# One post-norm transformer-like layer on one core: parameter load, table transposes, buffer slots, step order and last tile rearranged

## The chip, the cores and the metric

The kernel runs on one NeuronCore of one Trainium2 chip. The metric is the device time of one execution in microseconds; the time before is 1027.43 us, the median of three runs (1026.75 to 1028.75). Lower is better. All arithmetic is float32; large products are made from float32r parts (a value split in a high part and a residual, three matmuls for one product).

## The reference, cut to what matters

```python
h = x @ w_in                                  # 1024 x 1024 times 1024 x 2048, split in u, q, k, v, gate
bu = einsum(u, b_bar); states = associative_scan(lam_bar, bu)      # S5: 32 groups, 64 complex states
y  = gelu(Re(C . states) + d * u); y_s5 = rms_norm(y * sigmoid(y @ glu_w + glu_b))
y_ret = group_norm(retention(rotary(q), rotary(k), v)) * silu(gate)  # 4 heads, chunks of 64
x1 = layer_norm(alpha * x + concat(y_s5, y_ret) @ w_out)
a, g = split(x1 @ w_up); a = causal_conv3(a) + conv_b
out = layer_norm(alpha * x1 + (silu(a) * g) @ w_down)              # 1024 x 2816 times 2816 x 1024
```

The sequence has 1024 positions, the width is 1024, the channel mixer's inner width 2816.

## The kernel before, in words

The whole layer is one Python function that issues instructions to five engines: T (TensorE, "PE" in the profile), V (VectorE, DVE), S (ScalarE, ACT), G (GpSimd, POOL) and SP (the queue that issues nearly all DMAs). A planner orders each engine's instructions ahead of time: at each point of its own modelled run it takes the earliest instruction in program order whose inputs are ready, so an instruction can stand ahead of one that is earlier in the code. On the chip each engine then works through its list strictly in that order, with semaphores for the dependencies.

**Buffers.** Most SBUF tiles come from an arena of 20 narrow slots (2048 words per partition) and 2 wide ones. `A.get` takes the slot that was freed longest ago, `A.free` puts one at the end of the list. A tile in a used slot can be written only when every access to the tile that had the slot before is over. PSUM has eight banks, given out in turn by `bank`; `small` gives the same bank again as long as nothing else took one.

**First projection and S5 tables.** `project(blk, ...)` multiplies x by one quarter of w_in: four pairs `kp`, each loaded and split by `load_w` (lines 181 to 189: ACT makes the high part, DVE the residual), 24 matmuls per k-block. Block 0 gives u in eight banks; lines 286 to 295 copy u to U0 and U1 on ACT and store them to DRAM (`uscr`, line 294) in four DMAs; `load_UT` (line 299) reads them back transposed. Beside this DVE works out the S5 tables from the parameters: par3 (steps and eigenvalues, line 277) is loaded by `load_constants`, which `project(0)` calls after its second pair. Lines 326 to 407 are a long chain of small DVE operations on 32 to 256 columns; lines 421 to 423 make W0 and W1 from two products and a sum each, 2048 columns wide. Line 491 loads d over a part of `par` that line 422 reads.

**The second projection (v).** `project(2, ...)` multiplies by the block of v with seven banks, and between its matmuls it takes steps from a list, one per matmul: in the first two k-blocks (42 matmuls) eight `make_BT` steps, one every five matmuls, each with four transposes of W (line 451) into the one bank of `small` and a copy on ACT into BT0 or BT1 (line 452); in the next two eight `make_V` steps (line 465) with BT and UT. wsp2_0 and wsp2_1, the weights of the first two pairs, get their slots ahead of time; wsp2_2 takes whatever slot is next.

**Retention, gated unit, output product.** Lines 945 to 983 write the order of the steps by hand as strings: letter and block number. y is the S5 output, s, o, n and t the retention's scores, output, norm and transpose, a, m and b the gated unit's transposes in, product and transposes out, w the output product's retention part, F and f the two parts of the output product for blocks 4 to 7, p its second part for blocks 0 to 3. s, o, m, b, a, t, w, F take one to three banks each, in that order.

**Last product.** Line 1314 on: the second half of the output (zw[1], four tiles) is normalized by `layer_norm_far` on DVE while PE multiplies the last quarter for the four tiles of zw[0]: 33 matmuls of 512 columns for each tile, then line 1322 adds, and the tile is normalized. Tiles 0 and 1 use `layer_norm` (DVE, then ACT for the scale and GpSimd for adding the bias, line 867), tiles 2 and 3 `layer_norm_last` (two DVE operations of 512 columns, line 891, each with its own DMA). Each norm takes the power of the variance on GpSimd (line 860).

Of the kernel before, what the change touches and what calls it, by code (L numbers as in the profile page):

```python
# [12 lines left out]
F32 = mybir.dt.float32  # L13
F32R = mybir.dt.float32r
I32 = mybir.dt.int32
AF = mybir.ActivationFunctionType
ALU = mybir.AluOpType
# [3 lines left out]
P = 128  # L21
# [7 lines left out]
EPS = 1e-5  # L29
# [6 lines left out]
S_B1, S_B2, S_C1, S_C2, S_LRE, S_LIM, S_LS, S_END = 0, 512, 1024, 1536, 2048, 2080, 2112, 2144  # L36
# [70 lines left out]
def layer_kernel(ctx, tc, a, out):  # L107
    nc = tc.nc
    V, S, G, T, SP = nc.vector, nc.scalar, nc.gpsimd, nc.tensor, nc.sync

    cp = ctx.enter_context(tc.tile_pool(name="cp", bufs=1))
# [3 lines left out]
    A = Arena(ap_, 20, 2)  # L115
# [5 lines left out]
    def bank(name, keep=None):  # L121
        bank_n[0] += 1
        while bank_n[0] % 8 in kept.values():
            bank_n[0] += 1
        if keep is not None:
            kept[keep] = bank_n[0] % 8
        return ps.tile([P, 512], F32, tag=f"ps{bank_n[0] % 8}", name=name)
# [4 lines left out]
    def mm3(o, lh, ll, rh, rl, first, last):  # L132
        T.matmul(o, lhsT=lh, rhs=rh, start=first, stop=False)  # L133
        T.matmul(o, lhsT=lh, rhs=rl, start=False, stop=False)  # L134
        T.matmul(o, lhsT=ll, rhs=rh, start=False, stop=last)  # L135
# [31 lines left out]
    ahead_w = {}  # L167
# [27 lines left out]
    def project(blk, ops, banks, between=(), after=None, mid=None):  # L195


        ws = []
        late = len(between) > 0
        for kp in range(4):  # L200
            with tc.high_priority(0 if blk == 0 else HP):
                w, n = load_w(blk, kp)
            todo = deque(between[kp]) if late and kp < 2 else deque()
            ws.append(w)
            for q in range(2):
                k = 2 * kp + q
                if k < 7:
                    for (xi_, wi_) in ((0, 0), (0, 1), (1, 0)):
                        for j in range(7 if late and kp < 2 else 8):
                            l, r = ops(w[:, q], k, j, xi_, wi_)  # L210
                            T.matmul(banks[j], lhsT=l, rhs=r, start=(k == 0 and xi_ == 0 and wi_ == 0), stop=False)  # L211
                            if todo:
                                todo.popleft()()
                else:
                    for j in range(8):
                        proj3(banks[j], ops, w[:, q], k, j, False, True)
            assert not todo
            if mid is not None and kp == 1:
                mid()
            if late and kp < 2:  # L220
                if kp == 0:
                    continue
                if after is not None:
                    after()
                banks[7] = small("late")
                for k in range(4):
                    wk = ws[k // 2][:, k % 2]
                    proj3(banks[7], ops, wk, k, 7, k == 0, False)
                A.free(f"wsp{blk}_0")
            A.free(n)  # L230
            if blk == 3:
                A.free(f"x{2 * kp}", f"x{2 * kp + 1}")
# [11 lines left out]
    def spread_out(groups, n):  # L244

        return [g for gr in groups for g in [gr] + [lambda: None] * (n - 1)]
# [24 lines left out]
    banks = [bank(f"u{j}") for j in range(8)]  # L271
    par = A.get([P, 2048], F32, "par")
    pw = A.get([P, 2048], F32, "pw")
    par3 = pw[:, 1600:1696]

    def load_constants():
        SP.dma_start(par3, a["s5p"][:, 2048:S_END])
        SP.dma_start(con, a["con"])
        SP.dma_start(ident, a["ident"])
        SP.dma_start(par, a["s5p"][:, 0:2048])  # L280
        SP.dma_start(gains, a["gains"])
# [90 lines left out]
    l2, t5, kr, ki = tmp32(), tmp32(), tmp32(), tmp32()  # L372
# [40 lines left out]
    def vec_b(t, lo):  # L413
        return cust(t, lo * 16, [[16, 16], [0, 8], [1, 16]])

    A.free("scr")
    W = []
    for h in range(2):
        w_ = A.get([P, 16, 8, 16], F32, f"W{h}")
        t_ = A.get([P, 16, 8, 16], F32, f"Wt{h}")  # L420
        V.tensor_mul(w_, rev_pow(KR, 16 * h), vec_b(par[:, S_B1:S_B1 + 512], 16 * h))
        V.tensor_mul(t_, rev_pow(KIs, 16 * h), vec_b(par[:, S_B2:S_B2 + 512], 16 * h))
        V.tensor_add(w_, w_, t_)
        A.free(f"Wt{h}")
        W.append(w_)

    UT = []
    for h in range(2):
        UT.append(load_UT(h, f"UT{h}"))
        A.free(f"U{h}")  # L430

    scan = A.get([P, 4, 2, 256], F32, "scan")
    t1s = [scan[:, h] for h in range(2)]
# [13 lines left out]
    def make_BT(q):  # L447
        b_ = small(f"bt{q}")
        for e in range(4):
            g = 4 * q + e  # L450
            T.transpose(b_[:, e * P:(e + 1) * P], W[g // 16][:, g % 16].rearrange("p j c -> p (j c)"), ident)
        S.copy(BT[q // 4][:, 4 * (q % 4):4 * (q % 4) + 4], b_.rearrange("p (g k) -> p g k", g=4))
# [8 lines left out]
    def make_V(i):  # L461
        h, q = i // 4, i % 4
        b_ = small(f"v{h}{q}")
        for e in range(4):
# [4 lines left out]


    banks = [bank(f"v_{b}") for b in range(7)] + [None]
    project(2, ops_b, banks, [spread_out([partial(make_BT, q) for q in range(8)], 5),
                              spread_out([partial(make_V, i) for i in range(8)], 5)])
    A.free("BT0", "BT1", "UT0", "UT1")
    vt = [A.get([P, 4, 512], F32, f"vt{h}") for h in range(2)]
# [10 lines left out]
    def short_kernel(g):  # L486
        T.matmul(kb[:, 16 * g:16 * g + 16], lhsT=W[g // 16][:, g % 16].rearrange("p j c -> p (j c)"),
                 rhs=c1s[:, 16 * g:16 * g + 16], start=True, stop=True)
# [78 lines left out]
    banks = [bank(f"qk{b}") for b in range(7)] + [None]  # L567
# [28 lines left out]
    def glu_weights():  # L596
        r = A.get([P, 4, 512], F32, "glr")
        SP.dma_start(r, a["glu_w"])
        glh = A.get([P, 4, 512], F32R, "glh")
        gll = A.get([P, 4, 512], F32R, "gll")  # L600
        for k in range(4):
            S.copy(glh[:, k], r[:, k])
            V.tensor_sub(gll[:, k], r[:, k], f32(glh[:, k]))
        A.free("glr")
        return glh, gll

    glw = []
    banks = [bank(f"g_{b}") for b in range(8)]
    project(3, ops_b, banks, mid=lambda: glw.extend(glu_weights()))
    glh, gll = glw  # L610


# [124 lines left out]
    mh = cp.tile([P, 1], F32, name="mh")  # L737
# [125 lines left out]
    def layer_norm(z, lnv, pool, i):  # L863
        mv, rs = norm_stats(z, pool, i)
        V.scalar_tensor_tensor(z, z, mv[:, 0:1], lnv[:, 0], ALU.subtract, ALU.mult)
        S.activation(z, z, AF.Copy, scale=rs)  # L866
        G.tensor_add(z, z, lnv[:, 1])  # L867
# [18 lines left out]
    def layer_norm_last(z, lnv, pool, i, after):  # L886
        mv, rs = norm_stats(z, pool, i)
        V.scalar_tensor_tensor(z, z, mv[:, 0:1], lnv[:, 0], ALU.subtract, ALU.mult)
        for q in range(2):
            cs = slice(512 * q, 512 * q + 512)  # L890
            V.scalar_tensor_tensor(z[:, cs], z[:, cs], rs, lnv[:, 1, cs], ALU.mult, ALU.add)
            after(q, cs)
# [20 lines left out]
    def x1_transpose(b):  # L913
# [16 lines left out]
        if r:  # L930
# [7 lines left out]
    steps = {"y": s5_out, "s": ret_scores, "o": ret_out, "n": ret_norm, "t": ret_transpose, "a": glu_t, "m": glu_m,  # L938
             "b": glu_b, "w": out_ret, "F": out_first, "f": out_rest, "p": out_s5, "x": x1_transpose, "W": wo_load, "Z": z_load}

    def run(text):
        for step in text.split():
            steps[step[0]](int(step[1]))
# [12 lines left out]
    run("o2 t1 a0 s3 n2 m0 a1 o3 t2 m1 s4 n3 a2")  # L956
    A.free("qkT0", "vt0", "gt0")
    wo_split("wor", 0)
    run("m2 b0 o4 t3 a3 s5 n4 m3")
    A.free("y51")  # L960
    wo_split("wor", 1)
    z_load(0)
    run("b1 a4 w0 o5 t4 s6 n5 m4 b2 a5 w1 o6 t5 s7 n6 m5")
    z_load(1)
    run("b3 a6 w2 o7 t6 m6 b4 n7 a7")
    A.free("qkT1", "kz", "vt1", "gt1")
    wo_load("wos", 0)
    wo_load("wos", 1)
# [7 lines left out]
    lnv = A.get([P, 2, DM], F32, "ln1")  # L976
    SP.dma_start(lnv[:, 0], a["ln1_g"].partition_broadcast(P))
    SP.dma_start(lnv[:, 1], a["ln1_b"].partition_broadcast(P))
    run("t7 F4 b7 f4 F5 f5")
    A.free("vecs", "ptyr", "yTr0")  # L980
    mixctx.close()
    x1_slots(0)
# [151 lines left out]
    NP = NF // 2  # L1134
    wd, araw, araw_n, dops = {}, [], [0], {}
# [113 lines left out]
    zw = []  # L1249

    def outb(b):

        return out[16 * b:16 * b + 16].rearrange("p i d -> (p i) d")

    LO, HI = slice(0, 512), slice(512, 1024)
# [22 lines left out]
    for s_ in range(3):  # L1278
        banks = [[bank(f"dn{s_}{e}{i}") for i in range(4)] for e in range(2)]
# [27 lines left out]
        if s_ == 1:  # L1307
            lnv = A.get([P, 2, DM], F32, "ln2")
# [5 lines left out]
    for m in range(NP):  # L1314
        down_prep_last(m)
    layer_norm_far([zw[1][:, i] for i in range(4)], lnv, cp, lambda i: SP.dma_start(outb(4 + i), zw[1][:, i]))
    for i in range(4):
        b_ = bank(f"dn3{i}")
        for m in range(NP):
            down_mm(b_, *dops[3, m], i, m == 0, m == NP - 1)  # L1320
        z, cs = zw[0][:, i], slice(512, 1024)
        V.tensor_add(z[:, cs], z[:, cs], b_)
        if i < 2:
            layer_norm(z, lnv, cp, f"b{i}")
            SP.dma_start(outb(i), z)
        else:
            layer_norm_last(z, lnv, cp, f"b{i}", lambda q, cs: (SP, S)[q].dma_start(outb(i)[:, cs], z[:, cs]))


_ORDER = ["con", "ident", "xT", "xn", "w_in", "s5p", "d", "glu_w", "glu_b", "gains", "w_out",  # L1330
# [50 lines left out]
```

## Time and profile before

| | |
|---|---|
| median of three runs | 1027.43 us |
| profiled execution, its own time | 1028.04 us |
| its span, first to last instruction | 1026.3 us |
| mean granted TensorE clock | 0.993 |
| PE busy | 1004.3 us (98%) |
| DVE busy | 796.4 us (78%) |
| ACT busy | 447.7 us (44%) |
| GpSimd busy | 49.6 us (5%) |
| mean DMA rate over the span | 121 GB/s |

The span is what the profiler saw from the first to the last instruction; the execution's own time is 1.7 us longer. Busy time of an engine is the time in which an instruction of it was under way. All times in microseconds from the span's start.

### The profile page before, as it was taken

To read this page: it belongs to the slowest core of one execution; us is meant where nothing else is said; L and a number is where in the kernel's file an instruction comes from. 1 tells how busy PE (TensorE), PEld (TensorE's weight loads), DVE (VectorE), ACT (ScalarE), POOL (GpSimd) and SP (SyncE) were. 2 spreads that over 40 slices of the span, in tenths; PEclk is the share of its full clock that TensorE was granted. 3 is DMA by queue.
4 is the path that set the end of the run, shared out by engine and by line. 5 is a ranking of instruction groups with operands and counts; after the bars stand their busy time and mean duration, and the time that the engine had idled before them with its cause. 6 is when DMAs were issued, how large, how long until landed. Compare 5 with 4: busy or idle time off the path is not lost.

```text
span 1026.3 us, 12781 instructions
## 1 busy us (share of the span) xinstructions
PE 1004.3 (98%) x4748; PEld 828.7 (81%) x4748; DVE 796.4 (78%) x1376; ACT 447.7 (44%) x778; POOL 49.6 (5%) x60
## 2 busy tenths in 40 slices
PE   9989999999999999999999999999999999999996
PEld 7768887887777888788888888888888888888885
DVE  6937787727775599999878778778777896759987
ACT  4426302247562047554444444445444445444800
POOL 0000000002210150000000000000000000000003
PEclk9989999999999999999999999999999999999998
DMA  7362001261212223144232232322324996643113
GB/s 287 111 195 74 30 11 42 96 212 61 104 44 103 82 103 103 52 154 144 84 121 103 96 109 103 110 96 103 113 93 154 317 315 217 226 144 123 42 42 123
DMA packets 41934, 124.31 MB, mean 121 GB/s; under 512 B 4384, under 2 KB 10656, under 8 KB 37520
## 3 DMA queue, kind: packets, MB, share of 16 engines
q1 hardware_dynamic: 41584, 122.98, 34.4%
q8 instruction: 37, 0.61, 0.2%
q10 hardware_dynamic: 288, 0.52, 0.1%
q14 instruction: 25, 0.20, 0.1%
HBM read 92.32 MB, written 31.16 MB: 120 GB/s over the span
## 4 chain that ended last, share of the span: by engine, by line
PE 54%; DVE 5%; POOL 2%; issue 1%; DMA 1%; ACT 1%; POOLq 0%; DVEq 0%; SPq 0%
PE dn L134 6%; PE dn L135 6%; PE dn L133 6%; DVE ring L1007 1%; DVE XT L1234 1%; DMA wu<-in_w_up_dram 1%; POOL zw L867 1%; DMA wd<-in_w_down_dram 1%; POOL z L867 0%; DVE lbsf L877 0%; POOL lrsa L860 0%; DVE zw L1299 0%; POOL lrsb L860 0%; DVE zw L1306 0%; ACT z L866 0%
## 5 line engine op out<-in xcount | busy, mean ns | idle before, releaser
L1006 ACT CAST ring<-wu 128x512 fp32r<-128x512 f32 x130 | 80.0, 620 | 144.7 <-DMA wu<-in_w_up_dram 17.4
L1007 DVE TENSOR_TENSOR ring<-wu,ring 128x512 fp32r<-128x512 f32 x130 | 88.5, 687 | 21.4 <-ACT ring L1006 21.3
L134 PE MATMUL dn<-ring 128*128 128x512 f32 x264 | 102.9, 390 | 0.1
L135 PE MATMUL dn<-ring 128*128 128x512 f32 x264 | 102.8, 390 | 0.0
L133 PE MATMUL dn<-ring 128*128 128x512 f32 x264 | 102.8, 389 | 0.0
L1006 ACT CAST ring<-araw 128x512 fp32r<-128x512 f32 x66 | 41.1, 623 | 75.7 <-PE dn L134 61.8
L1007 DVE TENSOR_TENSOR ring<-araw,ring 128x512 fp32r<-128x512 f32 x66 | 45.3, 688 | 26.9 <-ACT ring L1006 26.9
L134 PEld LDWEIGHTS dn<-ring 128*128 128x128 f32 x264 | 49.6, 188 | 10.8 <-DVE ring L1007 0.5
L133 PEld LDWEIGHTS dn<-ring 128*128 128x128 f32 x264 | 49.6, 188 | 10.4
L135 PEld LDWEIGHTS dn<-ring 128*128 128x128 f32 x264 | 49.6, 188 | 10.1
L186 ACT CAST wsp<-wraw 128x512 fp32r<-128x512 f32 x32 | 19.1, 618 | 67.0 <-issue 49.7
L1007 DVE TENSOR_TENSOR ring<-wd,ring 128x512 fp32r<-128x512 f32 x66 | 44.9, 686 | 1.0 <-ACT ring L1006 1.0
L187 DVE TENSOR_TENSOR wsp<-wraw,wsp 128x512 fp32r<-128x512 f32 x32 | 21.4, 687 | 30.9 <-ACT wsp L186 30.8
L1006 ACT CAST ring<-wd 128x512 fp32r<-128x512 f32 x66 | 40.5, 617 | 7.8 <-DVE wd L1172 4.4
L211 PE MATMUL v<-wsp,x 128*128 128x512 f32 x147 | 41.3, 417 | 0.0
L211 PE MATMUL g<-wsp,x 128*128 128x512 f32 x168 | 40.1, 394 | 0.6 <-ACT qkT L589 0.6
L211 PE MATMUL u<-x,wsp 128*128 128x512 f32 x168 | 38.6, 391 | 0.6 <-ACT x L162 0.6
L211 PEld LDWEIGHTS u<-x,wsp 128*128 128x128 f32 x168 | 31.4, 188 | 8.0 <-ACT x L162 1.6
L211 PE MATMUL qk<-wsp,x 128*128 128x512 f32 x147 | 36.9, 395 | 0.0
L211 PEld LDWEIGHTS g<-wsp,x 128*128 128x128 f32 x168 | 30.8, 188 | 7.2 <-ACT qkT L589 1.3
L211 PEld LDWEIGHTS qk<-wsp,x 128*128 128x128 f32 x147 | 27.2, 188 | 6.4 <-ACT vt L477 0.9
L211 PEld LDWEIGHTS v<-wsp,x 128*128 128x128 f32 x147 | 27.8, 199 | 4.9
(1142 smaller groups left out, 2687.6 us busy)
## 6 DMA issues: line engine op xcount, KB each, us to landing
wu<-in_w_up_dram SPq DMA_DIRECT2D x22, 1024.0 KB, 4.9
araw<-hd SPq DMA_DIRECT2D x33, 512.0 KB, 3.8
wraw<-in_w_in_dram SPq DMA_DIRECT2D x32, 256.0 KB, 3.3
hd<-cg SPq DMA_DIRECT2D x22, 256.0 KB, 2.0
hd<-cg SPq DMA_DIRECT2D x11, 512.0 KB, 2.6
hd<-sS SPq DMA_DIRECT2D x11, 512.0 KB, 2.8
wd<-in_w_down_dram SPq DMA_DIRECT2D x11, 512.0 KB, 5.6
wd<-in_w_down_dram SPq DMA_DIRECT2D x22, 256.0 KB, 6.0
```

Source lines behind the costliest of these rows:

```text
L133: T.matmul(o, lhsT=lh, rhs=rh, start=first, stop=False)
L134: T.matmul(o, lhsT=lh, rhs=rl, start=False, stop=False)
L135: T.matmul(o, lhsT=ll, rhs=rh, start=False, stop=last)
L186: S.copy(t[:, q, 0], r)
L187: V.tensor_sub(t[:, q, 1], r, f32(t[:, q, 0]))
L211: T.matmul(banks[j], lhsT=l, rhs=r, start=(k == 0 and xi_ == 0 and wi_ == 0), stop=False)
L867: G.tensor_add(z, z, lnv[:, 1])
L1006: S.copy(t[:, 0], src)
L1007: V.tensor_sub(t[:, 1], src, f32(t[:, 0]))
L1234: V.tensor_sub(lo[:, ks], src[:, ks], f32(hi[:, ks]))
```

## The change

Five edits. (1) `project` calls its `mid` after each of the first two pairs, with the pair's number; `load_constants` loads par3 after the first pair and the rest after the second, as before; `project(3)`'s call still acts only after the second. (2) W0 and W1 share one temporary tile Wt. (3) wsp2_2 gets its slot ahead of time, before U0 and U1 are freed; both U tiles are freed together after that. (4) In `project(2)` the first ten places of the step list are empty and `make_BT` steps follow every four matmuls instead of every five. (5) The hand-written step order puts the gated unit's b steps (and one f) later, behind output products and transposes, and a7 earlier. (6) In the last product, tiles 0 to 2 use `layer_norm_last` with their DMAs all on SP; tile 3 is multiplied in two quarters of 256 columns, with statistics per quarter, and written in three pieces.

```diff
-            if mid is not None and kp == 1:
-                mid()
+            if mid is not None and kp < 2:
+                mid(kp)
...
-    def load_constants():
-        SP.dma_start(par3, a["s5p"][:, 2048:S_END])
+    def load_constants(kp):
+        if kp == 0:
+            SP.dma_start(par3, a["s5p"][:, 2048:S_END])
+            return
...
+    t_ = None
     for h in range(2):
         w_ = A.get([P, 16, 8, 16], F32, f"W{h}")
-        t_ = A.get([P, 16, 8, 16], F32, f"Wt{h}")
+        if h == 0:
+            t_ = A.get([P, 16, 8, 16], F32, "Wt")
...
-        A.free(f"Wt{h}")
         W.append(w_)
+    A.free("Wt")
     for h in range(2):
         UT.append(load_UT(h, f"UT{h}"))
-        A.free(f"U{h}")
+    ahead_w["wsp2_2"] = A.get([P, 2, 2, 512], F32R, "wsp2_2")
+    A.free("U0", "U1")
...
-    project(2, ops_b, banks, [spread_out([partial(make_BT, q) for q in range(8)], 5),
+    project(2, ops_b, banks, [[lambda: None] * 10 + spread_out([partial(make_BT, q) for q in range(8)], 4),
...
-    project(3, ops_b, banks, mid=lambda: glw.extend(glu_weights()))
+    project(3, ops_b, banks, mid=lambda kp: glw.extend(glu_weights()) if kp == 1 else None)
...
-    run("m2 b0 o4 t3 a3 s5 n4 m3")
+    run("m2 o4 t3 b0 a3 s5 n4 m3")
...
-    run("b1 a4 w0 o5 t4 s6 n5 m4 b2 a5 w1 o6 t5 s7 n6 m5")
+    run("a4 w0 b1 o5 t4 s6 n5 m4 a5 w1 b2 o6 t5 s7 n6 m5")
...
-    run("b3 a6 w2 o7 t6 m6 b4 n7 a7")
+    run("a6 w2 b3 o7 a7 t6 m6 b4 n7")
...
-    run("t7 F4 b7 f4 F5 f5")
+    run("t7 F4 b7 F5 f4 f5")
...
-    for i in range(4):
+    for i in range(3):
         b_ = bank(f"dn3{i}")
         for m in range(NP):
             down_mm(b_, *dops[3, m], i, m == 0, m == NP - 1)
-        z, cs = zw[0][:, i], slice(512, 1024)
-        V.tensor_add(z[:, cs], z[:, cs], b_)
-        if i < 2:
-            layer_norm(z, lnv, cp, f"b{i}")
-            SP.dma_start(outb(i), z)
-        else:
-            layer_norm_last(z, lnv, cp, f"b{i}", lambda q, cs: (SP, S)[q].dma_start(outb(i)[:, cs], z[:, cs]))
+        z = zw[0][:, i]
+        V.tensor_add(z[:, HI], z[:, HI], b_)
+        layer_norm_last(z, lnv, cp, f"b{i}", lambda q, cs: SP.dma_start(outb(i)[:, cs], z[:, cs]))
+    z = zw[0][:, 3]
...
+    Q = [slice(256 * q, 256 * q + 256) for q in range(4)]
+    for q in range(2):
+        V.bn_stats(bs[:, q], z[:, Q[q]])
+    for q in (2, 3):
+        b_ = bank(f"dn33{q}")[:, 0:256]
+        for m in range(NP):
+            (lh, ll), (rh, rl) = dops[3, m]
+            ts_, cs = slice(3 * P, 4 * P), Q[q - 2]
+            mm3(b_, lh[:, ts_], ll[:, ts_], rh[:, cs], rl[:, cs], m == 0, m == NP - 1)
+        V.tensor_add(z[:, Q[q]], z[:, Q[q]], b_)
+        V.bn_stats(bs[:, q], z[:, Q[q]])
+    V.bn_aggr(mv, bs)
+    V.tensor_scalar(rs, mv[:, 1:2], EPS, None, ALU.add)
+    G.tensor_tensor(rs, rs, mh, ALU.pow)
+    for q in range(4):
+        V.scalar_tensor_tensor(z[:, Q[q]], z[:, Q[q]], mv[:, 0:1], lnv[:, 0, Q[q]], ALU.subtract, ALU.mult)
+    for q, cs in enumerate((LO, Q[2], Q[3])):
+        V.scalar_tensor_tensor(z[:, cs], z[:, cs], rs, lnv[:, 1, cs], ALU.mult, ALU.add)
+        (SP, S, SP)[q].dma_start(outb(3)[:, cs], z[:, cs])
```

## Rows read from the trace of the kernel before

**Rows 1.** The page's first part: busy time and share of the span, each engine.

```profile
PE 1004.3 (98%) x4748; PEld 828.7 (81%) x4748; DVE 796.4 (78%) x1376; ACT 447.7 (44%) x778; POOL 49.6 (5%) x60
```

**Rows 2.** Waits of PE: line waiting, releaser, us in total, times, longest.

```profile
PE bt L451 <- ACT BT L452: 3.1, 2, 2.6
PE bt L451 <- issue: 2.4, 1, 2.4
PE yst L775 <- ACT ptyr L723: 1.4, 2, 0.9
...
PE wb L133 <- ACT yTs L779: 0.7, 1, 0.7
PE glu L133 <- ACT gTs L749: 0.6, 1, 0.6
```

**Rows 3.** Windows: busy us (count) of each engine, PEclk, DMA share, GB/s.

```profile
50.00:60.00 10.00, 7.01 (x33) 5.15 (x32) 9.62 (x25) 1.89 (x4) 0.00 (x0) 0.83 0.86 245
```

**Rows 4.** Timeline of PE, 49 to 72: start, us, line, count.

```profile
49.34 1.07 PE L211 MATMUL v<-wsp,x 128*128 128x512 f32 x4
...
57.63 0.60 PE L451 MATMUL bt<-ident,W 128*128 128x128 f32 x4
...
59.00 0.60 PE L451 MATMUL bt<-ident,W 128*128 128x128 f32 x4
...
71.88 1.05 PE L465 MATMUL v<-UT,BT 128*128 128x128 f32 x8
```

**Rows 5.** Timeline of ACT, 44 to 63.

```profile
44.78 5.35 ACT L293 COPY U<-u 128x512 f32<-128x512 f32 x8 [7.38 <-PE u L251]
...
61.68 1.14 ACT L186 CAST wsp<-wraw 128x512 fp32r<-128x512 f32 x2 [2.82 <-DMA uscr<-U]
```

**Rows 6.** Timeline of SP's queue, 50 to 58.

```profile
50.58 0.33 SPq L491 DMA_DIRECT2D par<-in_d_dram  x1
50.96 4.88 SPq L294 DMA_DIRECT2D uscr<-U  x4
57.12 0.36 SPq L299 DMA_DIRECT2D UT<-uscr  x1
```

**Rows 7.** Timeline of DVE, 10 to 53; in brackets the idle time before and its releaser.

```profile
10.35 1.23 DVE L163 TENSOR_TENSOR x<-xraw,x 128x1024 fp32r<-128x1024 f32 x1 [2.06 <-ACT x L162]
...
15.49 0.18 DVE L329 TENSOR_SCALAR scr<-pw 128x32 f32<-128x32 f32 x1
...
46.06 4.49 DVE L422 TENSOR_TENSOR Wt<-pw,par 128x2048 f32<-128x2048 f32 x2
50.47 4.49 DVE L423 TENSOR_TENSOR W<-W,Wt 128x2048 f32<-128x2048 f32 x2
```

**Rows 8.** Timelines of PE and of ACT around two retention blocks.

```profile
250.54 0.71 PE L688 MATMUL o<-st,qkT 64*128 64x128 f32 x8
...
259.78 0.50 PE L133 MATMUL glu<-glh,gTs 128*128 128x512 f32 x1
...
251.69 1.14 ACT L723 ACTIVATE ptyr<-o,rs 128x128 f32<-128x128 f32 x3
...
264.19 1.14 ACT L723 ACTIVATE ptyr<-o,rs 128x128 f32<-128x128 f32 x3
```

**Rows 9.** Tile last: count, ns min/median/max, first and last start.

```profile
L135 PE MATMUL dn<-last x44: 387/389/390, 987.3 to 1016.5; 128*128 128x512 f32 x44
```

**Rows 10.** Tile zw in the tail, the same columns.

```profile
L1322 DVE TENSOR_TENSOR zw<-zw,dn x4: 669/675/681, 1002.8 to 1018.2; 128x512 f32<-128x512 f32 x4
L891 DVE SCALAR_TENSOR_TENSOR zw<-zw,lrsb,ln x4: 746/748/751, 1016.8 to 1022.4; 128x512 f32<-128x512 f32 x4
...
L867 POOL TENSOR_TENSOR zw<-zw,ln x2: 2391/2838/3285, 1008.9 to 1013.9; 128x1024 f32<-128x1024 f32 x2
```

**Rows 11.** Timelines of DVE and of GpSimd in the tail.

```profile
1016.83 1.41 DVE L891 SCALAR_TENSOR_TENSOR zw<-zw,lrsb,ln 128x512 f32<-128x512 f32 x2 [3.34 <-POOL lrsb L860]
...
1020.22 1.46 POOL L860 TENSOR_TENSOR lrsb<-lrsb,mh 128x1 f32<-128x1 f32 x1 [3.42 <-DVE lrsb L859]
```

More of the change, by code (lines that the diff above doesn't have):

```diff
@@ L1320, in layer_kernel @@
             down_mm(b_, *dops[3, m], i, m == 0, m == NP - 1)
-        z, cs = zw[0][:, i], slice(512, 1024)
-        V.tensor_add(z[:, cs], z[:, cs], b_)
-        if i < 2:
-            layer_norm(z, lnv, cp, f"b{i}")
-            SP.dma_start(outb(i), z)
-        else:
-            layer_norm_last(z, lnv, cp, f"b{i}", lambda q, cs: (SP, S)[q].dma_start(outb(i)[:, cs], z[:, cs]))
+        z = zw[0][:, i]
+        V.tensor_add(z[:, HI], z[:, HI], b_)
+        layer_norm_last(z, lnv, cp, f"b{i}", lambda q, cs: SP.dma_start(outb(i)[:, cs], z[:, cs]))
+    z = zw[0][:, 3]
+    bs = cp.tile([P, 4, 6], F32, name="ebs")
+    mv = cp.tile([P, 2], F32, name="emv")
+    rs = cp.tile([P, 1], F32, name="ers")
+    Q = [slice(256 * q, 256 * q + 256) for q in range(4)]
[17 more added lines that the diff above has]
+        (SP, S, SP)[q].dma_start(outb(3)[:, cs], z[:, cs])
 _ORDER = ["con", "ident", "xT", "xn", "w_in", "s5p", "d", "glu_w", "glu_b", "gains", "w_out",
```

## The prediction

> **What bounds the kernel now.** I read the page's first part first: TensorE (PE) is busy 1004.3 of a span of 1026.3 us [rows 1]. So no other engine's load is worth anything by itself; only the 22 us in which PE stands still, or runs at half clock, can come back. Second, the waits with PE as the waiting engine [rows 2]: the table transposes (line 451) wait 3.1 + 2.4 us, the largest item by far; the gated unit's transposes (line 775) 1.4, its products on gTs 0.6, the output product on yTs 0.7. Third, the windows [rows 3]: in the stretch that holds these transposes the granted clock is 0.83; the ten microseconds after it show the same 0.83, and the rest of the span 1.00. A mean of 0.83 between levels 1.0 (2.4 GHz) and 0.5 (1.2 GHz) is a third of the time, 3.4 us, at 1.2 GHz, which costs 1.7 us in each of the two. Fourth, the timelines of that stretch, engine by engine [rows 4 to 7]. The rest of the idle time is the start and the tail behind PE's last matmul.
>
> **Front: the table transposes.** Before, v starts at 49.34 and make_V's first matmul comes at 71.88 [rows 4], 22.5 us later. The work in between is 42 matmuls of project(2) at 0.227 us ((1016.5 - 987.3) / 43 / 3 from the groups of the last products, [rows 9]) and 8 transpose groups; from 57.63 to 59.00 a group and four matmuls take 1.37 [rows 4], so a group costs 1.37 - 0.91 = 0.46. Sum 9.5 + 3.7 = 13.2. So 9.3 us are lost here: 5.5 waits [rows 2], the rest the half clock.
>
> Where they come from: (a) the first group waits 2.4 [rows 2] for W0, whose sum (line 423) starts at 50.47 as the first of two [rows 7]; (b) a later group waits 2.6 us because ScalarE's copy of its predecessor stands in ScalarE's queue behind the cast of wsp2_2, which starts at 61.68 after waiting for the U stores [rows 5], since wsp2_2 lies in U1's slot; (c) the stores themselves start at 50.96, directly behind the load of d [rows 6], although the copies that they store run from 44.78 [rows 5]. That load overwrites the part of par that both line 422 products read, and these end at 50.47 [rows 7]. SP's queue is in order, so the d load held four stores back.
>
> What the change does there: eleven matmuls ahead of the first group put it at 49.34 + 11 x 0.227 = 51.8. With one Wt the DVE order becomes mul, mul, mul, add W0, mul, add W1: W0's sum, which ended at 50.5 + 2.2 = 52.7, ends one 2.2 us operation earlier; against that stand 1.3 us for the two residuals of wsp2_2, which in scr's slot no longer wait for U and now fall among the W operations. Early parameters: DVE is in order and had only 2.06 us idle ahead of 10.35 before its first parameter operation at 15.49 [rows 7], so the chain can start at most about 2 us earlier; I take 1.3, two thirds of it. They shift the DMAs behind them on SP by one issue, 0.5 us, hidden by the 48 matmuls (10.9 us) of the first two blocks; without that cover it costs 0.5. So W0 is ready near 52.7 - 2.2 + 1.3 - 1.3 = 50.5, ahead of 51.8, and (a) is gone. (b) is gone as well.
>
> New: BT0 takes U0's slot and BT1 takes U1's (I followed the first-in first-out list of slots; before, BT0 had Wt1's, BT1 U0's). So the first copy must wait until both U0 stores have landed, and the fifth until U1's have. Behind that copy waits the next group on PE, since all groups share one bank. The second line 422 product, and with it the d load, is now free later: 50.47 + 2.2 + 1.3 - 1.3 = 52.7. All depends on how many stores the planner puts ahead of the d load. Before, it took the load to be free just ahead of the first store; the load is now 2 us later in the chain, and the four copies finish 1.3 us apart (5.35 us for 8, [rows 5]), which puts the load near the second store. If both U0 stores go ahead, at 46.2 and 47.5, they land at about 52.6 (before, UT0's load followed the first two by 57.12, within 6.2 us of 50.96 and with all four under way [rows 6]): no wait for the first copy. U1's stores then go at 53 and land near 58.6, where the fifth group (51.8 + 4 x 1.37 = 57.3) has its copy due at 57.9: about 1 us with its queue. Lower end 0, upper end 3.4 (2.6 as the wait of before, and half clock after it). I take 9.3 - 1.3 = **8.0 gained**. UT0's load is then issued before 55 and lands 7 later, make_V is due near 63.9.
>
> The Trainium skill, DMA: Bandwidth & Descriptors ("Where the ~2 µs actually goes"), says that a semaphore wait happens on the issuing sequencer ahead of dispatch and not in the DMA engines. By that rule the d load holds whatever stands behind it also now, which is the first rival below; the rows on SP agree.
>
> **Middle: the retention blocks.** Gone: 1.4 (b0 and b1 now stand behind other work), 0.6 (a7 comes ahead of t6 and m6), 0.7 (F5 ahead of f4 gives yTs 5.4 us): 2.7. New, by counting the eight banks round: o4 now takes the bank of o3's second half, which n3's activations free. These run from 251.69 for 1.14 us, while o4 ran at 250.54 [rows 8]. So o4 waits 2.3 us, with m2, the next products, waiting for a cast on ScalarE behind the same activations; b0's transposes (0.4) can fill. Net loss 1.9, bounds 0 (the planner finds other work) and 2.3 plus 1.7 of half clock. Sum: **0.8 gained**, bounds -1.3 and 2.7. m3 takes o4's bank and waits for n4; 24 matmuls of w0 (5.4 us) hide that, and what it costs without them stands under the rivals. The other moved steps find the same kind of predecessor in their bank as before.
>
> **Tail.** PE's last matmul starts at 1016.5 [rows 9] and ends 0.4 later, but the last add (line 1322) starts only at 1018.2 [rows 10]: DVE's line 891 for the tile before waited 3.3 us [rows 11] for a power on GpSimd, which stood behind the adds of line 867 (2.4 to 3.3 us each [rows 10]). These adds go. In their place DVE gets four more line 891 of 0.70 and the quarter's add and statistics (0.35 each, half of a 512-wide 0.68). From 1002.8, the first line 1322, DVE was busy 15.4 - 3.3 = 12.1; with 2.7 + 0.7 it is 15.5, so the last quarter's add starts at 1018.3, where it was. PE's tile of 66 matmuls of 256 columns instead of 33 of 512: lower bound half of 0.227 each (no change), upper bound 0.227 each (+7.5); 0.12 taken, half plus the small part that does not shrink: +0.4, hidden behind DVE. The Trainium skill, TensorE: Matmul & The Clock Gate (LDWEIGHTS), prices a load of 128 columns at 128 / 1.2 = 107 ns; by that the 66 pairs would be just hidden, and no run here has shown a 256-column product at full clock.
>
> From that add to the end: before 0.68 add, 0.69 statistics, 0.5 aggregate and epsilon, 1.6 until the power (1.46 [rows 11]) is there, 1.4 line 891, ending 1023.1 (1022.4 + 0.75, [rows 10]), and 3.2 for the write. After: 0.35 + 0.35 + 0.5 + 1.6 (the four quarter products lie beside it) + 0.75 + 0.4 + 0.4 = 4.35, ending 1022.6. **0.6 gained**; bounds 1.4 (DVE keeps up and starts at 1017.4) and a loss as large as PE's excess less 1.4.
>
> **Sum.** 8.0 + 0.8 + 0.6 = 9.4. The profiled execution took 1028.04 (span 1026.3 and 1.7 around it), 0.6 above the median of the timed runs, 1027.43. So 1018.6 on its own scale, 1018.0 as a median.
>
> **Rivals.** *The d load stays ahead of a U0 store (35%).* Then that store goes at 53 and lands at 57.5; the first copy waits, PE stands from 53.3 to 58.2, and 1.7 of half clock follows: make_V at 49.3 + 13.2 + 4.9 + 1.7 = 69.1, later by the slower groups, 69.8. Gain 2.1 in place of 8.0: **1023.9**. For it: the load was ahead of all four before. Against: two more operations now precede it.
> *All four stores stay behind it and the early parameters bring nothing (7%).* The load is free at 54.0, U0 lands at 60.6, PE stands from 53.3 for 8 us, plus 1.7: make_V at 72.2, and the change of the front does nothing. Left: -0.3 + 0.8 + 0.6: **1026.3**.
> *The bank round (slower side, 6%).* If m3 stands ahead of w0 in PE's order it waits for n4's end at 265.3, from 259.78 on [rows 8]: 5.5, with o4's 2.3 and 1.7 of half clock after each 11.2, against 2.7 removed: the middle loses 8.5. With the front at 8.0 this is 1027.3; it decides as soon as the front gives less than 7.9, and at 2.1 the time is **1033.2**.
> The forecast has 52%.
>
> **How the numbers follow.** The low end is the forecast with the front's whole 9.3 and most of the middle's 2.7: 1015. The high end takes in most of the first rival: 1025. A difference of 0.2%, 2 us, is what a measurement of this kernel can tell. Faster by that (below 1025.4): the forecast's 52% and nine tenths of the first rival's 35%, less a little: 0.82. Within it: the second rival, a tenth of the first, part of the bank round: 0.13. Slower: 0.05.
>
> **What would show it.** Right: no wait of line 451 over 1 us, granted clock near 1.0 between 50 and 70, make_V's first matmul at 63 to 65, UT0 issued before 55; o4 waiting for line 723; the final add near 1018 less what was gained. Wrong: the d load issued between the stores of U0 (first rival), a long PE wait of line 451 on line 452 near 53; line 133 waiting on line 723; PE's last tile longer than 8 us.

## The result and the profile after

| | before | after |
|---|---|---|
| median (runs, lowest to highest) | 1027.09 us (4, 1025.42 to 1028.75) | 1016.66 us (4, 1016.30 to 1016.77) |
| profiled execution, its own time | 1028.04 us | 1016.30 us |
| its span | 1026.3 us | 1014.5 us |
| mean granted TensorE clock | 0.993 | 0.998 |

The ratio is 0.9898, with a 95% interval from 0.9881 to 0.9915: 10.4 us faster by the medians, where 9.4 was forecast. The two profiled executions lie 11.7 apart, since that of before lay 0.95 above its median and that of after 0.36 below. Lines have higher numbers after the change: table transposes 456 (451 before), BT copy 457, make_V 470, d load 496, U stores 296, UT loads 301, n's activations 728 (723).

The changed kernel's first part of the page (PE busy 99% of a span shorter by 11.8) and PE's waits, to be held against [rows 1, 2]:

```profile
PE 1002.4 (99%) x4781; PEld 829.6 (82%) x4781; DVE 798.1 (79%) x1387; ACT 445.1 (44%) x776; POOL 45.1 (4%) x58
```

```profile
PE warm L267 <- DVE zero L264: 1.2, 1, 1.2
PE up1C L1060 <- DVE ring L1012: 0.8, 1, 0.8
PE wo L133 <- ACT ptyr L728: 0.7, 2, 0.5
PE g L211 <- ACT qkT L594: 0.6, 1, 0.6
PE s L674 <- DVE vecs L765: 0.5, 1, 0.5
```

All five waits of [rows 2] are gone. One is new, 0.7 of the output product on ptyr. Next the windows of the table stage (busy us and count of PE, PEld, DVE, ACT, POOL; then granted clock, DMA share, GB/s) and the timelines of PE, of ScalarE and of SP's queue:

```profile
50.00:60.00 10.00, 10.00 (x57) 8.08 (x56) 9.52 (x23) 3.72 (x7) 0.00 (x0) 1.00 0.99 320
60.00:70.00 10.00, 10.00 (x64) 8.61 (x63) 1.13 (x3) 3.46 (x9) 0.00 (x0) 1.00 0.16 64
```

```profile
49.76 2.66 PE L211 MATMUL v<-wsp,x 128*128 128x512 f32 x11
52.26 0.60 PE L456 MATMUL bt<-ident,W 128*128 128x128 f32 x4
52.61 1.18 PE L211 MATMUL v<-wsp,x 128*128 128x512 f32 x4
53.63 0.60 PE L456 MATMUL bt<-ident,W 128*128 128x128 f32 x4
...
63.24 1.06 PE L470 MATMUL v<-UT,BT 128*128 128x128 f32 x8
```

```profile
45.20 5.36 ACT L295 COPY U<-u 128x512 f32<-128x512 f32 x8 [1.57 <-PE u L251]
52.94 0.59 ACT L457 COPY BT<-bt 128x512 f32<-128x512 f32 x1 [2.38 <-PE bt L456]
```

```profile
46.49 4.45 SPq L296 DMA_DIRECT2D uscr<-U  x4
52.23 4.80 SPq L301 DMA_DIRECT2D UT<-uscr  x2
57.11 0.42 SPq L496 DMA_DIRECT2D par<-in_d_dram  x1
```

The clock stays at 1.00, the level of 2.4 GHz, where [rows 3] had 0.83. The groups follow at 1.37 us without a gap, as forecast. On SP the four stores no longer wait behind the d load: it now stands behind them and both UT loads. make_V starts at 63.24 in place of 71.88 [rows 4]: 8.6 gained. From the tile of the last products (count, ns, first and last start) the rest can be read, against 987.3 to 1016.5 in [rows 9]:

```profile
L135 PE MATMUL dn<-last x55: 279/389/389, 976.8 to 1006.5; 128*128 128x512 f32 x33, 128*128 128x256 f32 x22
```

The first start is 10.5 earlier, the last 10.0, the end of the span 11.8. So the middle gained 10.5 - 8.6 = 1.9, and the tail 11.8 - 10.5 = 1.3: 0.5 lost on PE's quarters, 1.8 won behind them. DVE's end of the tail:

```profile
1007.21 0.40 DVE L1344 TENSOR_TENSOR zw<-zw,dn 128x256 f32<-128x256 f32 x1
1007.64 0.43 DVE L1345 BATCH_NORM_STATS2 ebs<-zw 128x6 f32<-128x256 f32 x1
...
1008.47 1.67 DVE L1350 SCALAR_TENSOR_TENSOR zw<-zw,emv,ln 128x256 f32<-128x256 f32 x4
1010.05 1.54 DVE L1352 SCALAR_TENSOR_TENSOR zw<-zw,ers,ln 128x512 f32<-128x512 f32 x3
```

The last add starts 0.7 after the start of PE's last product; before, it was 1.7 (1018.2 and 1016.5, [rows 9, 10]).

### The profile page after: what moved, and what is told of

It reads as the page before. It is cut to its first block, busy times and chain, and to the rows that moved or that the text cites. A ratio compares the mean times of both kernels' runs of the same rounds, so it can differ in the third digit from the quotient of the medians.

```text
span 1014.5 us, 12859 instructions
## 1 busy us (share of the span) xinstructions
PE 1002.4 (99%) x4781; PEld 829.6 (82%) x4781; DVE 798.1 (79%) x1387; ACT 445.1 (44%) x776; POOL 45.1 (4%) x58
## 4 chain that ended last, share of the span: by engine, by line
PE 55%; DVE 6%; POOL 1%; ACT 1%; DMA 1%; issue 1%; DVEq 0%; SPq 0%; POOLq 0%
PE dn L134 6%; PE dn L133 6%; PE dn L135 6%; DVE XT L1239 1%; DVE ring L1012 1%; DMA wu<-in_w_up_dram 1%; DVE zw L888 0%; POOL z L872 0%; DVE zw L896 0%; DVE lbsf L882 0%; DVE zw L887 0%; POOL lrsa L865 0%; DVE lbsb L862 0%; DVE zw L1304 0%; DVE zw L1311 0%
## 5 line engine op out<-in xcount | busy, mean ns | idle before, releaser
L134 PEld LDWEIGHTS dn<-ring 128*128 128x128 f32 x264 | 49.5, 188 | 10.4 <-DVE ring L1012 0.3
L133 PEld LDWEIGHTS dn<-ring 128*128 128x128 f32 x264 | 49.5, 188 | 10.4
L1104 DVE SCALAR_TENSOR_TENSOR cg<-Ab,cv,cg 128x1024 f32<-128x1024 f32 x22 | 28.2, 1284 | 4.7 <-ACT cg L1103 4.5
```

Source lines behind the costliest of these rows:

```text
L1104: V.scalar_tensor_tensor(c, Ab[:, 1:1025], cv[:, f, 1:2], c, ALU.mult, ALU.add)
```

## The experiments

Times are medians; the kernel before had 1027.12, 1027.76, 1026.95 and 1027.18 us in the four series. Its runs spread over 4 us (1024.99 to 1028.94 in the first series), so traces, each of one execution, place what the medians only bound.

**The three parts alone.** The change has six numbered edits. e1 is the kernel before with edits 1 to 4, e2 with edit 5 (the four strings), e3 with edit 6.

> Kernel before with edits 1 to 4 alone (parameters, one Wt, wsp2_2's slot, step spacing). Theory (the front holds 8.6 us: in the changed kernel make_V's first matmul came at 63.24 in place of 71.88): 1018.5 us, between 1018.0 and 1019.0. Rival (the front is worth the 8.0 of the prediction and the rest comes from an interplay of the three parts): 1019.1 or more.

> Kernel before with edit 5 alone (the hand-written step order). Theory (the planner puts other work into the wait of o4, so that nearly all of the 2.7 us of waits comes back): 1025.0 us, no PE wait over 0.8 us in the retention stretch but one of up to 2.1 in total on ptyr, line 723. Rival (the prediction's term of 0.8): 1026.3.

> Kernel before with edit 6 alone (last tile in two quarters, no GpSimd additions). Theory (DVE keeps up with PE, the tail behind PE's last matmul shrinks by 1.8 while PE's tile grows by 0.4): 1025.7 us. Rival (the prediction's 0.6: DVE is still the one that comes late): 1026.5.

| | median us | ratio to before, interval |
|---|---|---|
| e1 | 1019.75 | 0.9928, 0.9915 to 0.9941 |
| e2 | 1024.72 | 0.9977, 0.9968 to 0.9985 |
| e3 | 1025.43 | 0.9984, 0.9975 to 0.9992 |

That is 7.4, 2.4 and 1.7 us. Their sum, 11.5, is 1.1 more than the whole, within the intervals (about 1 us each); an interplay isn't needed. e1's median missed its theory by 0.7 and falls to the rival's side (1019.1 or more), while its trace is on the theory's: make_V at 63.11, and in the groups of the last products of e1 and of e2

```profile
L135 PE MATMUL dn<-last x44: 388/389/389, 978.8 to 1008.0; 128*128 128x512 f32 x44
```

```profile
L135 PE MATMUL dn<-last x44: 388/389/389, 984.2 to 1013.4; 128*128 128x512 f32 x44
```

e1 stands 8.5 ahead of before there. The 1.1 between trace and median is mostly the 0.9 by which the profiled execution of before lay above its median. Part of that lies in the front itself: e2, e3 and e11 have the front of before, and their make_V starts at

```profile
70.95 1.05 PE L465 MATMUL v<-UT,BT 128*128 128x128 f32 x8
...
71.19 1.05 PE L465 MATMUL v<-UT,BT 128*128 128x128 f32 x8
...
70.90 1.05 PE L465 MATMUL v<-UT,BT 128*128 128x128 f32 x8
```

against 71.88 in [rows 4]. Held against these, the changed kernel's 63.24 is 7.7 to 8.0 ahead, not 8.6. e2 stands 3.1 ahead, of which 0.9 was there at make_V (70.95), before any step that it changes: 2.2 for the order. Its waits of lines 775, 779 and 749 are gone, and one of 0.6 on ptyr has come. In e3's trace the last product starts at 1015.9 and the span ends at 1023.9, 8.0 later, as in the changed kernel; before it was 9.8.

**e4: the stores leave SP's queue.** One word in the kernel before:

```diff
-            SP.dma_start(bass.AP(ud.tensor, ud.offset + (2 * h + c) * P * 1024, [[P, P], [16 * 1024, 8], [1, P]]),
+            S.dma_start(bass.AP(ud.tensor, ud.offset + (2 * h + c) * P * 1024, [[P, P], [16 * 1024, 8], [1, P]]),
```

> Kernel before with one change: the four U stores are issued by ScalarE's own queue, right behind the copies that they store, and no longer stand behind the load of d on SP. Theory (the load of d, waiting for line 422, holds the stores and through them wsp2_2's cast and the BT copy behind it): the stores go at 46 to 50 in place of 51 to 56, PE's wait of 2.6 on BT goes with part of the half clock behind it, W0's wait of 2.4 stays: 1023 to 1024.5 us. Rival (that cast is late for another reason, its own load or the residuals on DVE): 1027, the wait of 2.6 unchanged.

1023.87 us, ratio 0.9966 (0.9953 to 0.9978): 3.2 gained, as the theory says. ScalarE issues the four stores from 46.70 to 50.77, and only one wait of the transposes is left:

```profile
59.44 1.14 ACT L186 CAST wsp<-wraw 128x512 fp32r<-128x512 f32 x2 [1.67 <-DMA uscr<-U]
60.48 0.58 ACT L452 COPY BT<-bt 128x512 f32<-128x512 f32 x1
```

The cast is 2.2 earlier than in [rows 5] but still in the way, so the wait is 1.7, not 0 (the last store was issued more than 4 us earlier; why its landing took longer isn't shown). W0's wait is gone against the expectation, because the new order has 20 products ahead of the first group. That the d load held the stores, and they the cast, is shown; its share of the 3.2 isn't separated from that of the new order.

**e5 to e8: each front edit taken back from the changed kernel.** Edit 1 (par3 loaded after the second pair again), edit 2 (two Wt), edit 3, and edit 4, of which 2 and 3 are in short

```diff
...
-        if h == 0:
-            t_ = A.get([P, 16, 8, 16], F32, "Wt")
+        t_ = A.get([P, 16, 8, 16], F32, f"Wt{h}")
...
-    ahead_w["wsp2_2"] = A.get([P, 2, 2, 512], F32R, "wsp2_2")
-    A.free("U0", "U1")
+        A.free(f"U{h}")
```

> Changed kernel with edit 1 taken back: par3 is loaded behind the second pair again; the d load still stands behind all four U stores on SP. Theory (the early load moved W's products 1.15 us, and W0 would now be ready near 52.2 where the first group is due at 52.3): 1016.7 to 1017.2 us, a wait of line bt of 0 to 0.5. Rival (the 1.3 of the prediction is needed whole, W0 late by it): 1018 or more.

> Changed kernel with edit 2 taken back: W0 and W1 have a temporary tile each, and DVE does four products ahead of the two sums. Theory (W0 is ready one product later, 51.0 + 2.3 = 53.3, where the first group is due at 52.3): one wait of line bt of about 1.0, perhaps part of it half clock: 1017.7 to 1018.5 us. Rival (the shared tile matters only for where slots come free): 1016.7.

> Changed kernel with edit 3 taken back: wsp2_2 takes whatever slot is next, and its casts stand between BT copies on ScalarE again; the d load stays behind the U stores. Theory (the cast was late only because the stores were): the stores go at 46 to 51, the cast finds its slot free, W0 comes 1.3 earlier without the residuals: 1016.5 to 1017.3 us and no wait of line bt over 0.5. Rival (the prediction's point (b), the slot itself): a wait of 2.6 comes back, 1019.3 or more.

> Changed kernel with edit 4 taken back: the first table group stands at the head of the second projection and groups follow every five matmuls. Theory (W0 is ready at 51.0, the first group would be due at 50.0): a wait of line bt of about 1.1, 1017.8 us. Rival (planner or clock make more of it, as the 2.4 of the kernel before with half clock behind it): 1019 or more.

| | median us (lowest to highest) | ratio to before |
|---|---|---|
| e5 without edit 1 | 1016.91 (1015.93 to 1018.24) | 0.9894, 0.9877 to 0.9911 |
| e6 without edit 2 | 1018.30 (1017.82 to 1020.06) | 0.9912, 0.9896 to 0.9927 |
| e7 without edit 3 | 1018.50 (1017.87 to 1019.26) | 0.9910, 0.9896 to 0.9925 |
| e8 without edit 4 | 1016.35 (1016.19 to 1018.19) | 0.9894, 0.9879 to 0.9909 |

All four keep the d load behind the stores. The changed kernel was not timed again in their series; e5 and e8 end where it did (1016.66), and e6 and e7 lie 1.4 to 2.2 above those two, with ranges that overlap by less than half a microsecond. e5: as expected. e6: the size is as expected, the reason is not. Its ScalarE timeline:

```profile
45.40 4.00 ACT L295 COPY U<-u 128x512 f32<-128x512 f32 x6 [9.28 <-PE u L251]
52.17 0.62 ACT L186 CAST wsp<-wraw 128x512 fp32r<-128x512 f32 x1 [2.77 <-DVE W L425]
52.69 1.06 ACT L295 COPY U<-u 128x512 f32<-128x512 f32 x2
```

By the list of slots wsp2_2 now lies in the slot of the first Wt, which W0's sum reads until 52.1; its cast waits for that, with two U copies and so two banks of v behind it. PE waits 1.8 on U, and W0 isn't late. e7: the cast is on time, as the theory said, but a wait comes all the same:

```profile
52.13 0.60 PE L455 MATMUL bt<-ident,W 128*128 128x128 f32 x4
52.48 1.18 PE L211 MATMUL v<-wsp,x 128*128 128x512 f32 x4
55.66 0.66 PE L455 MATMUL bt<-ident,W 128*128 128x128 f32 x4 [2.00 <-ACT BT L456]
```

Here BT0 takes Wt's slot, which W1's sum uses until 54.9 (52.62 + 2.29), and the first copy comes at 55.02. Theory and rival both fail: the wait is that of BT0's slot. e8: theory and rival both fail. The first group runs at 50.78 without waiting, since W0 is ready at 50.67 (48.38 + 2.29), 0.1 ahead in this execution: the empty places bought nothing by themselves.

**e9: edit 1 alone** on the kernel before.

```diff
...
+        if kp == 0:
+            SP.dma_start(par3, a["s5p"][:, 2048:S_END])
+            return
...
```

> Kernel before with edit 1 alone: par3 is loaded one pair earlier. The order of SP's queue turns round with it: the d load now stands behind all four U stores and both UT loads. Theory (the order on SP is worth more than the earlier chain itself): the stores go from 46, the wait of 2.6 on BT is gone as in the kernel with the stores on ScalarE, W0's wait falls by 1.1: 1022.5 to 1024 us. Rival (only the chain's 1.1 us counts): 1026.

1022.46 us, ratio 0.9958 (0.9945 to 0.9971): 4.5 gained. The stores now go ahead of the d load, and wsp2_2's cast waits for them only 0.16 and starts at 58.08, 3.6 earlier than in [rows 5]:

```profile
48.44 4.43 SPq L296 DMA_DIRECT2D uscr<-U  x4
...
61.60 0.42 SPq L493 DMA_DIRECT2D par<-in_d_dram  x1
```

What is left on PE is

```profile
PE bt L453 <- ACT BT L454: 1.1, 1, 1.1
```

from BT0 in the second Wt's slot. W0's wait, of which 1.3 was to stay, is gone as well, but only because v starts 2.4 later in this execution than before, when W0 is nearly ready (52.3):

```profile
51.70 1.07 PE L211 MATMUL v<-wsp,x 128*128 128x512 f32 x4
52.61 0.60 PE L453 MATMUL bt<-ident,W 128*128 128x128 f32 x4
```

The W products start at 40.23 (40.94 before [rows 7]: 0.7 earlier), so most of the 4.5 is not the chain. The rival's 1026 is out.

**e10: a store held back.** In the changed kernel:

```diff
-            SP.dma_start(bass.AP(ud.tensor, ud.offset + (2 * h + c) * P * 1024, [[P, P], [16 * 1024, 8], [1, P]]),
-                         t[:, c])
+            if (h, c) != (0, 1):
+                SP.dma_start(bass.AP(ud.tensor, ud.offset + (2 * h + c) * P * 1024, [[P, P], [16 * 1024, 8], [1, P]]),
+                             t[:, c])
+        if h == 0:
+            U0 = t
...
     A.free("Wt")
+    SP.dma_start(bass.AP(ud.tensor, ud.offset + P * 1024, [[P, P], [1, 16]]), W[0][:, 15, 7])
+    SP.dma_start(bass.AP(ud.tensor, ud.offset + P * 1024, [[P, P], [16 * 1024, 8], [1, P]]), U0[:, 1])
```

> Changed kernel with a small transfer of 16 columns of W0 put on SP behind the first U store; it waits for W0's sum (51.0), so that the other three U stores stand behind it as they would have behind the d load, the second one of U0 last of all. Theory (the first rival of the prediction: BT0 lies in U0's slot, its copies wait until U0's stores have landed): a long wait of line bt on BT's copy, 4 to 5 us, half clock behind it: make_V near 69, 1022.5 us. Rival (a store held to 53 still lands ahead of what needs it): 1016.7 to 1017.5.

1021.32 us, ratio 0.9942 (0.9929 to 0.9956): 4.7 slower than the changed kernel. SP, ScalarE and PE:

```profile
46.66 0.38 SPq L297 DMA_DIRECT2D uscr<-U  x1
50.61 0.34 SPq L433 DMA_DIRECT2D uscr<-W  x1
51.00 1.05 SPq L297 DMA_DIRECT2D uscr<-U  x2
54.03 0.36 SPq L434 DMA_DIRECT2D uscr<-U  x1
```

```profile
58.28 0.59 ACT L462 COPY BT<-bt 128x512 f32<-128x512 f32 x1 [7.57 <-DMA uscr<-U]
```

```profile
52.77 3.92 PE L211 MATMUL v<-wsp,x 128*128 128x512 f32 x16
58.92 0.66 PE L461 MATMUL bt<-ident,W 128*128 128x128 f32 x4 [2.22 <-ACT BT L462]
```

Three stores stood behind one waiting transfer, and the first copy waited 7.57 us for the landing; the clock was 0.83 from 60 to 70. Not all of the hold is the queue's order: the small transfer waited 3.6 for W0's sum, and then the second store of U0, which writes the same part of uscr, 1.9 more for the small transfer to land. It went at 54.03, near the 53 of the rival. The order put 16 products into the gap in place of four, so PE itself waited 2.2. make_V came 7.0 later (70.19), but with those products done; at the last products 4.7 was left. That supports the first rival's mechanism (a U0 store that goes at 53 or 54 holds the first copy); in the changed kernel itself no store was held.

**e11: the norms without the quarters** on the kernel before.

```diff
-        if i < 2:
-            layer_norm(z, lnv, cp, f"b{i}")
-            SP.dma_start(outb(i), z)
+        if i < 3:
+            layer_norm_last(z, lnv, cp, f"b{i}", lambda q, cs: SP.dma_start(outb(i)[:, cs], z[:, cs]))
...
```

> Kernel before with half of edit 6: tiles 0 to 2 use layer_norm_last and write from SP, the last tile stays one product of 512 columns. Theory (the additions on GpSimd held DVE back 3.3 us, the last add started 1.3 us behind PE's last product; without them it starts within 0.5 of it): 0.8 of the 1.3 us of the whole edit, 1026.3 us. Rival (the quarters alone give it, since the GpSimd wait was hidden): 1027.1.

1026.25 us, ratio 0.9989 (0.9979 to 0.9999). In the trace DVE's wait of 3.3 [rows 11] is 0.4, the last product starts at 1015.7, the last add at 1016.60 and the span ends at 1024.7, 9.0 after that product (9.8 before): 0.8, as expected. The other 0.5 net are the quarters: 1.0 behind PE, less 0.5 on PE.

**e12: edits 1 and 4 both taken back** from the changed kernel.

> Changed kernel with edits 1 and 4 both taken back (late par3, old step spacing); edits 2 and 3, the step order and the tail stay. Each of the two alone cost nothing. Theory (edits 2 and 3 carry the front; W0 is ready near 51.3 and the first group due at 50.8): a wait of line bt of at most 0.6, 1016.5 to 1017.5 us. Rival (each stood in for the other: W0 late by the 0.5 to 1.2 of the late load with no empty places to cover it, and half clock behind that wait): 1018 to 1019.5.

1017.68 us (1017.35 to 1018.41), ratio 0.9910 (0.9893 to 0.9927): 1.0 above the changed kernel, whose runs ended at 1016.77. The time lies between theory and rival; two waits of the transposes are there, 0.7 on W0 (ready at 51.6, its group due at 50.8) and 0.5 on the first copy, which waited for U0's stores, and the stage from v to make_V takes 15.0 (13.5 in the changed kernel) with the clock at 1.00. Each edit covers for the other's absence, for a microsecond.

## Why the prediction was right, and where its sum was short

| term | forecast | by the traces of before and after | by the medians of e1, e2, e3 |
|---|---|---|---|
| front | 8.0 | 8.6 | 7.4 |
| middle | 0.8 | 1.9 | 2.4 |
| tail | 0.6 | 1.3 | 1.7 |
| sum | 9.4 | 11.8 | 11.5 (10.4 for the whole change) |

The middle and the tail gave more than the forecast by either measure. For the front that isn't clear, since the trace of before was late there (make_V at 71.88, 70.90 to 71.19 in e2, e3 and e11).

**Front.** The accounting was right: 13.2 for work alone, and the stage took 13.5 (49.76 to 63.24). What failed is "about 1 us with its queue", the 1.3 for the fifth group's copy. It rested on "which puts the load near the second store". The load went behind all four stores and the UT loads, so U1's stores were issued by 51 and no copy waited for them. v's start, 0.4 later than before, takes back part; it lay between 48.91 and 51.70 over the traces, so that isn't the change's. That the 8.0 came so near is partly luck: the 9.3 lost was read from a trace that was 0.7 to 1.0 later here than three others with the same front, and the 1.3 taken off was for a wait that didn't come. The block itself is shown by e4, e9 and e10. Why the load moved: it is still ahead of the stores with edit 5 or 6 alone (e2, e3), and behind them with edit 1 alone (e9) and in e5 and e12, which lack edit 1 and have 2 and 3. So edit 1 is enough, and so are 2 and 3 together with 5 and 6; no run separates 2 from 3. That the planner's own times do this is argued, not shown.

In e10 the transfer of W0's columns, issued at 50.61 when the sum ended, was followed at 51.00 by two stores, the first of which had its copies since 49.4 (six of eight that took 5.35 from 45.36). The Trainium skill, DMA: Bandwidth & Descriptors ("Where the ~2 µs actually goes"), puts a semaphore wait on the issuing sequencer; these rows agree.

**Early parameters.** "I take 1.3" failed in its place: the first parameter operation came at 15.32 (15.49 before, 15.11 in e5 without the edit). W's products started 1.15 earlier than before (39.79), and W0 was ready at 51.0, near the forecast's 50.5. But their start scatters: 39.37 to 40.32 in the seven traces with the edit, 40.05 to 40.94 in the seven without it, 0.5 apart in the mean, so the edit's own part is nearer 0.5. In the changed kernel this made nothing by itself (e5), nor did the eleven products ahead of the first group (e8); only without both is W0 late (e12). On the kernel before, the edit's worth was that it turned SP's order round (e9); in the changed kernel the order is turned without it too (e5).

**Slots.** Point (b), that wsp2_2's slot made the cast late, was right for the kernel before. For the changed kernel the prediction counted the slots right but not what the two edits do to each other: the shared Wt without the reserved slot puts BT0 into Wt's slot (e7, 1.8 us), the reserved slot without the shared Wt puts wsp2_2 there (e6, 1.6).

**Middle.** 2.7 was removed as forecast. "So o4 waits 2.3 us" failed. The planner took o4 apart, one bank at a time:

```profile
242.08 0.71 PE L693 MATMUL o<-st,qkT 64*128 64x128 f32 x4
242.72 0.71 PE L697 MATMUL o<-vt,ptyr 128*128 128x128 f32 x4
243.36 0.66 PE L702 MATMUL st<-vt,kz 128*64 128x128 f32 x8
243.94 0.55 PE L780 MATMUL yst<-ident,vecs 128*128 128x128 f32 x3
244.43 0.71 PE L693 MATMUL o<-st,qkT 64*128 64x128 f32 x4
```

n3's three activations ran from 243.24 for 1.14, and only o4's second half, at 244.43, stands right behind their end. Its first half, st and b0's transposes filled the time: the forecast's own bound, "0 (the planner finds other work)". What remains is the 0.7 of the output product on ptyr: 2.7 - 0.7 = 2.0, near the 1.9. The slower rival's m3 wait did not come.

**Tail.** "So the last quarter's add starts at 1018.3" failed: DVE needed 14.7 from its first add (992.54 to 1007.21), not 15.5, and came 0.4 behind PE's end (1006.54 + 0.28) where it had been 1.3 behind. That is near the forecast's better bound, in which DVE keeps up: 1.4, and 1.3 was seen. Besides, the last write took 2.9 (from 1011.59, the end of line 1352, to 1014.5) where 3.2 was counted before and after; and the forecast's own ends, 1023.1 and 1022.6, make its term 0.5, not 0.6. PE's share was right: 66 products from 998.75 to 1006.54, 0.120 apart. The trace shows each weight load at 187 to 192 ns, overlapping its neighbours, so the loads did hide. The Trainium skill (TensorE: Matmul & The Clock Gate, LDWEIGHTS) gives 107 ns for a load of 128 columns; here the trace's longer time decides.

**Rivals.** The first rival's place was wrong and its price of 5.9 a little high: 4.7 in e10, where the planner filled part of the wait. Of the signs of being right, all of the front came (clock, make_V at 63 to 65, UT0 by 55); o4's wait and the late add did not. Two signs of being wrong came in small: line 133 waited on the activations of ptyr, for 0.7 in place of 5.5, and PE's last tile took 8.1 (998.75 to 1006.82), just over the 8 named.

## What to carry to other kernels

In a queue that issues in order, look for a transfer that waits and count what stands behind it; a small edit far upstream can turn the order round and be worth more than the time it saves itself. When tiles share slots by a first-in first-out list, recount who inherits which slot after each edit: edits 2 and 3 look independent, but either one without the other put a tile into a slot still in use and cost 1.6 to 1.8 us. Where a planner reorders, a wait on one of two banks is an upper bound.

## What the runs showed of the hardware that was not expected

The first products after the start run slowly for a time that differs between runs. Groups of the first projection between 8 and 9 us, in the changed kernel and in e9 (count, busy us, mean ns):

```profile
L211 PE MATMUL u<-x,wsp 128*128 128x512 f32 x6 | 1.5, 392 | 0.0
```

```profile
L211 PE MATMUL u<-x,wsp 128*128 128x512 f32 x4 | 1.9, 628 | 0.0
```

The clock column shows 1.00 for both. From 5 to 10 us the traces hold between 10 (e9) and 21 products (e11), and v starts between 51.70 and 48.91 accordingly. Why is open; it is as large as several of the effects here, which is why a stage should be compared from its own start as well (the front: 22.5 before, 13.5 after).

A short wait doesn't always cost clock: a PE wait of 2.00 (e7) left it at 1.00, one of 1.84 (e6) and one of 2.22 (e10) had 0.83 in the windows where they lay or that followed, a third of ten microseconds at 1.2 GHz. In the front of the kernel before, the first two ten-microsecond windows from 50 on had 0.83 both in before and e11, but only the second in e2 and e3. The kernel before, with such waits in all four of these traces, spread over 4 us in 26 runs; the changed one over 0.5 in four, but e5 and e8, with none, over 2.3 and 2.0 in five, so the waits are not shown to be the cause of the spread.
